# Where the transposes of a batched score kernel keep their PSUM buffers, and which engine empties which

## The chip, the cores and the metric

The kernel runs on one core of one Trainium2 chip. The time is the device time of one execution in microseconds, and the median over several executions counts. Shorter is better. The names of the engines in the profile: PE is the matrix engine (PEld its weight load), DVE the vector engine, ACT the scalar engine, POOL the GpSimd engine, SP the engine whose queue issues the transfers here.

## What is computed

```python
def reference(q: np.ndarray, k: np.ndarray) -> np.ndarray:
    scale = 1.0 / np.sqrt(q.shape[-1])
    return (np.einsum('bhqd,bhkd->bhqk', q, k) * scale).astype(np.float32)
```

q and k are f32 arrays of 8 batches, 8 heads, 512 rows and 64 columns, 8.4 MB each. The result has 8 x 8 matrices of 512 x 512 f32 scores, 67.1 MB.

## The kernel before

The work is cut into four units (`UNITS`) of two batches each. A unit's k and q arrive as one tile `big` of 128 partitions with 32 KB on each, by two transfers of 2 MB (line 78). `load_and_cast` turns each of the two into a bf16 tile `xb`, in two halves, on POOL (line 82). All four units' loads and casts stand in the program ahead of everything else. The pool of `big` tiles has three buffers, which the loads and the output tiles share in rotation: units 0 to 2 take buffers 0 to 2, unit 3 takes buffer 0 again, and the output tiles follow with 1, 2, 0 and so on. So the first output tile needs unit 1's casts to be over, the second unit 2's, and the third unit 3's; from the fourth on, each needs the store of three tiles before to have landed.

`transpose` brings the columns of k and q onto the partitions. It does so in eight groups for each unit, four for k (line 107) and four for q (line 116). A group is eight 128 x 128 transposes on PE into one PSUM tile `tp` (a pool of two), and then four copies of 64 x 512 out of it, in `rearrange` (line 95). The groups' copies go to DVE and ACT in turn. k ends up in `kT`; q ends up in `qz`, a tile padded with zeros, of which there are two for the whole kernel, cleared by DVE at the start (line 147). `transpose` is a generator: a group is five steps, one that issues the eight transposes and four that issue one copy each, 40 steps for a unit.

`scores` computes one output tile of 4 MB, the matrices of four heads of one batch: 16 matmuls of 128 x 512 (line 132), two to a PSUM tile `ps` of two banks (a pool of three), and eight evacuations, each of 128 x 1024, which multiply by the scale (`evacuate`). Of six evacuations three are on ACT (line 64) and three on DVE (line 66). Then SP stores the tile with one transfer (line 137). A unit has four such tiles (`TILES`), so there are 16 stores and 128 evacuations.

The first unit's transposes run by themselves, before any score. The next unit's are mixed into the current unit's scores by hand: after each evacuation the main loop takes one or two steps of the generator. In unit 0 it takes one step after each evacuation of the first tile and two in the later tiles; in the other units one, and two after every fourth evacuation.

Each engine executes its instructions in the order of the program (`keep_in_program_order`), and waits at one of them until what it needs is there. SP has all eight loads first, then the 16 stores.

Of the kernel before, what the change touches and what calls it, by code (L numbers as in the profile page):

```python
# [1 line left out]

# [5 lines left out]


@with_exitstack  # L10
def kernel(
    ctx: ExitStack,
    tc: tile.TileContext,
    q: bass.AP,
    k: bass.AP,
    out: bass.AP,
):

    nc = tc.nc
    B, H, S, D = q.shape
    scale = 1.0 / (D ** 0.5)
    P = 128
    UNITS = B // 2
    N = H
    M = P // (2 * H)  # L30
    R = S // M
    J = R // 2
    RO = 8
    U = S // RO
    JJ = J // RO
    IW = 8 // JJ
    TILES = N // 2

    f32 = mybir.dt.float32
    bf16 = mybir.dt.bfloat16  # L40

    q_r = q.rearrange("(v b) g (m j) d -> v (b g m) (j d)", b=2, j=R)
    k_r = k.rearrange("(v b) g (m j) d -> v (b g m) (j d)", b=2, j=R)
    out_r = out.rearrange("(v b) (t x h) (u i) k -> v (b t) (h u) x (i k)", b=2, x=2, h=2, i=RO)

    consts = ctx.enter_context(tc.tile_pool(name="consts", bufs=1))

    big_pool = ctx.enter_context(tc.tile_pool(name="big", bufs=3))
    bf_pool = ctx.enter_context(tc.tile_pool(name="bf", bufs=6))
    t_pool = ctx.enter_context(tc.tile_pool(name="t", bufs=2))  # L50
    tpsum_pool = ctx.enter_context(tc.tile_pool(name="tpsum", bufs=2, space=bass.MemoryType.PSUM))
    psum_pool = ctx.enter_context(tc.tile_pool(name="psum", bufs=3, space=bass.MemoryType.PSUM))


    pinned = tc.keep_in_program_order

    n_evac = 0
    n_tp = 0

    def evacuate(dst, src):  # L60
        nonlocal n_evac

        if n_evac % 6 in (0, 2, 3):
            pinned(nc.scalar.mul(out=dst, in_=src, mul=scale))  # L64
        else:
            pinned(nc.vector.tensor_scalar(out=dst, in0=src, scalar1=scale, scalar2=None,  # L66
                                           op0=mybir.AluOpType.mult))
        n_evac += 1

    def half(h):  # L70
        return slice(h * D, (h + 1) * D)

    def load_and_cast(v):

        xf = big_pool.tile([P, 2, 2, J * D], f32, name="big")
        both = []
        for x, src in enumerate((k_r, q_r)):
            nc.sync.dma_start(out=xf[:, x], in_=src[v].rearrange("p (s c) -> p s c", s=2))
        for x in range(2):
            xb = bf_pool.tile([P, J, 2, D], bf16, name="xb")  # L80
            for s in range(2):
                pinned(nc.gpsimd.tensor_copy(out=xb[:, :, s, :],  # L82
                                             in_=xf[:, x, s].rearrange("p (j d) -> p j d", j=J)))
            both.append(xb)
        return both

    def rearrange(tp, pattern, dst):

        nonlocal n_tp
        copy = (nc.vector.tensor_copy, nc.scalar.copy)[n_tp % 2]  # L90
        n_tp += 1
        for s in range(2):
            src = tp[half(s)].rearrange(pattern, n=N, h=2)
            for h in range(2):
                pinned(copy(out=dst(s, h), in_=src[:, h]))  # L95
                yield

    def transpose(v, kb, qb):


        kT = t_pool.tile([P, N, M, 2, J], bf16, name="kT")
        qz = qzs[v % 2]
        ts[v] = (kT, qz)
        for j0 in range(0, J, 8):
            tp = tpsum_pool.tile([P, 8, P], bf16, name="tp")
            for j in range(8):
                pinned(nc.tensor.transpose(out=tp[:, j, :], identity=identity,  # L107
                                           in_=kb[:, j0 + j].rearrange("p s d -> p (s d)")))
            yield
            yield from rearrange(tp, "d j (n h m) -> d h n m j",  # L110
                                 lambda s, h: kT[half(h), :, :, s, j0:j0 + 8])
        for i0 in range(0, RO, IW):
            tp = tpsum_pool.tile([P, IW, JJ, P], bf16, name="tp")
            for i in range(IW):
                for jj in range(JJ):
                    pinned(nc.tensor.transpose(out=tp[:, i, jj, :], identity=identity,  # L116
                                               in_=qb[:, RO * jj + i0 + i].rearrange("p s d -> p (s d)")))
            yield
            yield from rearrange(tp, "d i jj (n h m) -> d h i n m jj",
                                 lambda s, h: qz[half(h), i0:i0 + IW, :, h * U:(h + 1) * U]  # L120
                                 .rearrange("d i n (m s jj) -> d s i n m jj", s=2, jj=JJ)[:, s])

    def scores(v, t):

        kT, qz = ts[v]
        o = big_pool.tile([P, 2, RO, S], f32, name="big")
        for x in range(2):
            n = 2 * t + x
            for i in range(0, RO, 2):
                ps = psum_pool.tile([P, 2, S], f32, name="ps")  # L130
                for w in range(2):
                    pinned(nc.tensor.matmul(out=ps[:, w, :], lhsT=qz[:, i + w, n, :],  # L132
                                            rhs=kT[:, n].rearrange("d m s j -> d (m s j)"),
                                            start=True, stop=True))
                evacuate(o[:, x, i:i + 2, :], ps)
                yield
        nc.sync.dma_start(out=out_r[v, t], in_=o.rearrange("p x i k -> p x (i k)"))  # L137

    def take(steps, count):
        for _ in range(count):  # L140
            next(steps, None)

    identity = consts.tile([P, P], dtype=bf16)
    make_identity(nc, identity)
    qzs = [consts.tile([P, RO, N, P], bf16, name=f"qz{n}") for n in range(2)]
    for qz in qzs:
        nc.vector.memset(qz, 0.0)  # L147
    cast = [load_and_cast(v) for v in range(UNITS)]

    ts = {}  # L150
    for _ in transpose(0, *cast[0]):
        pass
    for v in range(UNITS):
        ahead = transpose(v + 1, *cast[v + 1]) if v + 1 < UNITS else iter(())
        for t in range(TILES):
            for n, _ in enumerate(scores(v, t)):

                take(ahead, 1 + (t > 0 if v == 0 else n % 4 == 3))
        for _ in ahead:
            pass  # L160


# [1 line left out]
_INS = ['q', 'k']  # L164
_OUTS = [((8, 8, 512, 512), 'float32')]


# [23 lines left out]
```

## Time and profile before

| | us |
|---|---|
| median of 7 executions | 203.06 (202.72 to 203.38) |
| the profiled execution | 203.25 |
| its span, from the first to the last instruction | 201.4 |
| DVE busy | 126.3 |
| PE busy | 101.5 |
| ACT busy | 100.6 |
| POOL busy | 30.5 |

The span lacks what lies around the instructions, so it is shorter than the time of the same execution. In the profile's rows of 40 digits each digit is one fortieth of the span, about 5 us, and 9 means busy for 90% or more of it; the DMA row is the mean over the core's 16 DMA engines. The DMA engines moved 83.97 MB in 5510 packets: 16.78 MB were read from the chip's memory and 67.11 MB written. In a row of the costliest groups stand the line, the engine, the operation and its shapes, the number of instructions, the busy time and the mean ns of one, and then the idle time ahead of them with what ended most of it. A line of the timeline has the start, the busy time, the engine and line, the operation, and in brackets the idle time ahead of it and what ended it.

### The profile page before, as it was taken

The page shows a single profiled execution, that of the slowest core. Times are in us where ns is not written, and L with a number is a line of the kernel's source. Part 1 is how long each engine was busy: PE and PEld are TensorE (multiplying, and loading weights), DVE is VectorE, ACT ScalarE, POOL GpSimd, SP SyncE. Part 2 cuts the span into 40 slices and gives each one's busy share as a digit, 9 for nine tenths or more (in the row PEclk, how much of TensorE's full clock was granted, in tenths as well). Part 3 has the DMA queues.
Part 4 walks back from the last instruction along what each step waited for, and adds up shares of the span by engine and source line. Part 5 has one row for each costly group of instructions (what it writes and reads, how often), then busy time and mean ns, then how long its engine had stood idle before and what let it go on. Part 6 is the DMA issues. An engine that isn't in the chain of part 4 may idle for free.

```text
span 201.4 us, 1456 instructions
## 1 busy us (share of the span) xinstructions
PE 101.5 (50%) x503; PEld 48.2 (24%) x512; DVE 126.3 (63%) x130; ACT 100.6 (50%) x129; POOL 30.5 (15%) x22
## 2 busy tenths in 40 slices
PE   0033366753868549484935554954765465710000
PEld 0033343321413224242412221421222121200000
DVE  6736659995988949796749796669456064530000
ACT  2016667795765775666758563775525341520000
POOL 1277777557000000000000000000000000000000
PEclk9999999999678996969699997599587858555555
DMA  6999999999999999999999999999999999999993
GB/s 208 442 426 426 433 436 426 416 397 439 423 433 431 431 426 429 436 426 426 439 429 426 426 439 426 426 433 429 433 433 436 416 429 429 433 426 436 433 429 153
DMA packets 5510, 83.97 MB, mean 417 GB/s; under 512 B 384, under 2 KB 384, under 8 KB 384
## 3 DMA queue, kind: packets, MB, share of 16 engines
q1 hardware_dynamic: 5504, 83.89, 98.0%
q8 instruction: 4, 0.07, 0.1%
q14 instruction: 2, 0.02, 0.0%
HBM read 16.78 MB, written 67.11 MB: 416 GB/s over the span
## 4 chain that ended last, share of the span: by engine, by line
DMA 42%; DVE 8%; PE 6%; ACT 2%; issue 1%; ACTq 0%; SPq 0%; DVEq 0%
DMA out_dram<-big 42%; DVE big L66 7%; PE ps L132 6%; ACT big L64 2%; DVE kT L95 1%; ACT qz L95 1%; PE tp L116 1%; ACTq L64 0%; SPq L137 0%; DVEq L66 0%
## 5 line engine op out<-in xcount | busy, mean ns | idle before, releaser
L132 PE MATMUL ps<-kT,qz 128*128 128x512 bf16 x247 | 83.5, 461 | 52.5 <-ACT big L64 35.3
L66 DVE TENSOR_SCALAR big<-ps 128x1024 f32<-128x1024 f32 x64 | 76.3, 1221 | 40.4 <-DMA out_dram<-big 28.2
L64 ACT ACTIVATE big<-ps 128x1024 f32<-128x1024 f32 x64 | 63.6, 1022 | 56.8 <-DMA out_dram<-big 29.1
L132 PEld LDWEIGHTS <-qz 128*128 128x128 bf16 x256 | 28.0, 112 | 96.1 <-issue 85.0
L82 POOL CAST xb<-big 128x2048 bf16<-128x2048 f32 x16 | 29.8, 1893 | 17.9 <-DMA big<-in_k_dram 9.7
L95 ACT COPY kT<-tp 64x512 bf16<-64x512 bf16 x32 | 18.5, 578 | 14.6 <-PE tp L107 14.3
L95 DVE COPY kT<-tp 64x512 bf16<-64x512 bf16 x32 | 22.0, 687 | 6.0 <-PE tp L107 5.6
L95 DVE COPY qz<-tp 64x512 bf16<-64x512 bf16 x32 | 22.0, 687 | 3.1 <-PE tp L116 2.7
L95 ACT COPY qz<-tp 64x512 bf16<-64x512 bf16 x32 | 18.5, 578 | 4.5 <-PE tp L116 4.1
L107 PE MATMUL tp<-identity,xb 128*128 128x128 bf16 x128 | 11.5, 248 | 16.9 <-POOL xb L82 12.4
L116 PE MATMUL tp<-identity,xb 128*128 128x128 bf16 x128 | 12.7, 262 | 6.2 <-DVE kT L95 3.2
L107 PEld LDWEIGHTS <-xb 128*128 128x128 bf16 x128 | 10.1, 113 | 21.0 <-POOL xb L82 12.7
L116 PEld LDWEIGHTS <-xb 128*128 128x128 bf16 x128 | 11.1, 120 | 10.8 <-issue 8.8
L147 DVE MEMSET qz<- 128x4096 uint32 x2 | 6.9, 3472 | 2.5 <-PEq L175 1.7
L95 ACT ACT_TABLE_LOAD x1 | 1.3, 1283 | 0.7 <-PEq L175 0.7
masks.py:199 POOL TENSOR_SCALAR_AFFINE_SELECT identity<-identity 128x128 bf16<-128x128 bf16 x1 | 0.3, 292 | 0.1
masks.py:197 POOL MEMSET identity<- 128x128 bf16 x1 | 0.2, 204 | 0.3 <-POOLq L175 0.3
L175 POOL MEMSET const-float32-0.0<- 128x1 f32 x1 | 0.1, 98 | 0.2 <-issue 0.2
L175 POOL MEMSET const-bfloat16-1.0<- 128x1 bf16 x1 | 0.1, 101 | 0.0
L175 POOL MEMSET const-uint8-127<- 128x1 uint8 x1 | 0.1, 101 | 0.0
L175 POOL MEMSET const-float32-1.0<- 128x1 f32 x1 | 0.1, 98 | 0.0
## 6 DMA issues: line engine op xcount, KB each, us to landing
out_dram<-big SPq DMA_DIRECT2D x16, 4096.0 KB, 21.2
big<-in_k_dram SPq DMA_DIRECT2D x4, 2048.0 KB, 19.3
big<-in_q_dram SPq DMA_DIRECT2D x4, 2048.0 KB, 24.3
```

Source lines behind the costliest of these rows:

```text
L64: pinned(nc.scalar.mul(out=dst, in_=src, mul=scale))
L66: pinned(nc.vector.tensor_scalar(out=dst, in0=src, scalar1=scale, scalar2=None, op0=mybir.AluOpType.mult))
L82: pinned(nc.gpsimd.tensor_copy(out=xb[:, :, s, :], in_=xf[:, x, s].rearrange("p (j d) -> p j d", j=J)))
L95: pinned(copy(out=dst(s, h), in_=src[:, h]))
L107: pinned(nc.tensor.transpose(out=tp[:, j, :], identity=identity, in_=kb[:, j0 + j].rearrange("p s d -> p (s d)")))
L116: pinned(nc.tensor.transpose(out=tp[:, i, jj, :], identity=identity, in_=qb[:, RO * jj + i0 + i].rearrange("p s d -> p (s d)")))
L132: pinned(nc.tensor.matmul(out=ps[:, w, :], lhsT=qz[:, i + w, n, :], rhs=kT[:, n].rearrange("d m s j -> d (m s j)"), start=True, stop=True))
L147: nc.vector.memset(qz, 0.0)
L175: nc = _bacc.Bacc("TRN2", target_bir_lowering=False, num_devices=1)
```

## The change

Six things are changed:

- The first unit's transposes use two pools: groups 0, 1, 4 and 5 take the two `tp` buffers as before, groups 2, 3, 6 and 7 take buffers of the scores' pool `ps`. All other units use `tp` alone.
- Two of every three evacuations go to ACT and one to DVE. With three `ps` buffers in rotation, a buffer is then always emptied by the same engine.
- In unit 0 the main loop takes two steps of the next unit's transposes after every evacuation, in the first tile too. The other units are as before.
- The first half of the first cast (k of unit 0) is done by DVE.
- The transposes of k and q go through one helper, `transposed`.
- The two PSUM pools are made in the other order.

```diff
--- before.py
+++ after.py
@@ -33,7 +33,6 @@
     RO = 8
     U = S // RO
     JJ = J // RO
-    IW = 8 // JJ
     TILES = N // 2
 
     f32 = mybir.dt.float32
@@ -48,8 +47,8 @@
     big_pool = ctx.enter_context(tc.tile_pool(name="big", bufs=3))
     bf_pool = ctx.enter_context(tc.tile_pool(name="bf", bufs=6))
     t_pool = ctx.enter_context(tc.tile_pool(name="t", bufs=2))
+    psum_pool = ctx.enter_context(tc.tile_pool(name="psum", bufs=3, space=bass.MemoryType.PSUM))
     tpsum_pool = ctx.enter_context(tc.tile_pool(name="tpsum", bufs=2, space=bass.MemoryType.PSUM))
-    psum_pool = ctx.enter_context(tc.tile_pool(name="psum", bufs=3, space=bass.MemoryType.PSUM))
 
 
     pinned = tc.keep_in_program_order
@@ -60,7 +59,7 @@
     def evacuate(dst, src):
         nonlocal n_evac
 
-        if n_evac % 6 in (0, 2, 3):
+        if n_evac % 3 < 2:
             pinned(nc.scalar.mul(out=dst, in_=src, mul=scale))
         else:
             pinned(nc.vector.tensor_scalar(out=dst, in0=src, scalar1=scale, scalar2=None,
@@ -79,8 +78,8 @@
         for x in range(2):
             xb = bf_pool.tile([P, J, 2, D], bf16, name="xb")
             for s in range(2):
-                pinned(nc.gpsimd.tensor_copy(out=xb[:, :, s, :],
-                                             in_=xf[:, x, s].rearrange("p (j d) -> p j d", j=J)))
+                copy = nc.vector.tensor_copy if v == x == s == 0 else nc.gpsimd.tensor_copy
+                pinned(copy(out=xb[:, :, s, :], in_=xf[:, x, s].rearrange("p (j d) -> p j d", j=J)))
             both.append(xb)
         return both
 
@@ -101,22 +100,29 @@
         kT = t_pool.tile([P, N, M, 2, J], bf16, name="kT")
         qz = qzs[v % 2]
         ts[v] = (kT, qz)
-        for j0 in range(0, J, 8):
-            tp = tpsum_pool.tile([P, 8, P], bf16, name="tp")
-            for j in range(8):
-                pinned(nc.tensor.transpose(out=tp[:, j, :], identity=identity,
-                                           in_=kb[:, j0 + j].rearrange("p s d -> p (s d)")))
+        W = 8
+
+        def transposed(rows):
+            if v == 0 and n_tp % 4 > 1:
+                tp = psum_pool.tile([P, W, P], bf16, name="ps")
+            else:
+                tp = tpsum_pool.tile([P, W, P], bf16, name="tp")
+            for w, row in enumerate(rows):
+                pinned(nc.tensor.transpose(out=tp[:, w, :], identity=identity,
+                                           in_=row.rearrange("p s d -> p (s d)")))
+            return tp
+
+        for j0 in range(0, J, W):
+            tp = transposed([kb[:, j0 + j] for j in range(W)])
             yield
             yield from rearrange(tp, "d j (n h m) -> d h n m j",
-                                 lambda s, h: kT[half(h), :, :, s, j0:j0 + 8])
+                                 lambda s, h: kT[half(h), :, :, s, j0:j0 + W])
+        IW = W // JJ
         for i0 in range(0, RO, IW):
-            tp = tpsum_pool.tile([P, IW, JJ, P], bf16, name="tp")
-            for i in range(IW):
-                for jj in range(JJ):
-                    pinned(nc.tensor.transpose(out=tp[:, i, jj, :], identity=identity,
-                                               in_=qb[:, RO * jj + i0 + i].rearrange("p s d -> p (s d)")))
+            tp = transposed([qb[:, RO * jj + i0 + i] for i in range(IW) for jj in range(JJ)])
             yield
-            yield from rearrange(tp, "d i jj (n h m) -> d h i n m jj",
+            yield from rearrange(tp.rearrange("p (i jj) c -> p i jj c", jj=JJ),
+                                 "d i jj (n h m) -> d h i n m jj",
                                  lambda s, h: qz[half(h), i0:i0 + IW, :, h * U:(h + 1) * U]
                                  .rearrange("d i n (m s jj) -> d s i n m jj", s=2, jj=JJ)[:, s])
 
@@ -155,7 +161,7 @@
         for t in range(TILES):
             for n, _ in enumerate(scores(v, t)):
 
-                take(ahead, 1 + (t > 0 if v == 0 else n % 4 == 3))
+                take(ahead, 2 if v == 0 else 1 + (n % 4 == 3))
         for _ in ahead:
             pass
 
```

## Prediction

> **What bounds the kernel now.** I read the page's DMA rows first, because the kernel moves 84 MB and does little arithmetic on it.
>
> ```profile
> DMA  6999999999999999999999999999999999999993
> q1 hardware_dynamic: 5504, 83.89, 98.0%
> DMA out_dram<-big 42%; DVE big L66 7%; PE ps L132 6%; ACT big L64 2%; DVE kT L95 1%; ACT qz L95 1%; PE tp L116 1%; ACTq L64 0%; SPq L137 0%; DVEq L66 0%
> ```
>
> The 16 DMA engines are busy in every slice from 5 us to 196 us and 98% over the span, while the busiest compute engine, DVE, has 63%. The chain of waits names stores and the evacuations released by a store's landing; it goes back only to 57.3 us, and a compute piece on it costs time only where the queue behind it ran dry. So the question is where the DMA engines do less than full work. The view by stretches (length, then PE, PEld, DVE, ACT, POOL busy, clock, DMA share, GB/s):
>
> ```profile
> 0.00:2.00 2.00, 0.00 (x0) 0.00 (x0) 0.34 (x1) 1.27 (x1) 0.70 (x6) 1.00 0.33 57
> 2.00:3.00 1.00, 0.00 (x0) 0.00 (x0) 1.00 (x1) 0.01 (x1) 0.00 (x0) 1.00 0.74 197
> 3.00:4.00 1.00, 0.00 (x0) 0.00 (x0) 1.00 (x1) 0.00 (x0) 0.00 (x0) 1.00 0.82 344
> 39.00:41.50 2.50, 1.71 (x12) 0.87 (x12) 2.44 (x4) 1.88 (x3) 2.19 (x2) 1.00 1.07 393
> ...
> 198.00:199.00 1.00, 0.00 (x0) 0.00 (x0) 0.00 (x0) 0.00 (x0) 0.00 (x0) 0.50 0.23 98
> 199.00:200.00 1.00, 0.00 (x0) 0.00 (x0) 0.00 (x0) 0.00 (x0) 0.00 (x0) 0.50 0.12 49
> 200.00:201.40 1.40, 0.00 (x0) 0.00 (x0) 0.00 (x0) 0.00 (x0) 0.00 (x0) 0.50 0.00 0
> ```
>
> Front: 2 x 0.67 + 0.26 + 0.18 = 1.8 us of idle before the queue is full. Middle: nothing idle; one dip at 39 to 41.5 us, where the queue turns from loads to stores (393 GB/s against 428 to 431 in the long stretches: 2.5 x (1 - 393/428) = 0.2 us). End: 0.77 + 0.88 + 1.40 = 3.05 us with few or no engines. A share of 0.12 is two engines of 16: most are done at about 198.3 us, two go on to 200. So the span is 1.8 + about 196.5 of transfer + 3.1 = 201.4, and the profiled execution, 203.25 us, has 1.85 us around it.
>
> The two late engines can be traced back. In the trace's landing records all 16 engines report a load within 0.8 us of each other up to 33 us. For the last q load fifteen report at 42.3 to 43.2 us and one at 45.1. It fell behind at 36.6 to 39 us, where another queue takes time on one engine:
>
> ```profile
> q1 hardware_dynamic: 79, 1.03, 94.2%
> q8 instruction: 1, 0.02, 2.6%
> ```
>
> In that window, 36.4 to 39 us, an instruction fetch of one packet takes 0.026 x 16 x 2.6 = 1.1 us of one engine. That engine was already the last by 0.5 us, loses 1.2 us here and 0.85 us more at the turn to stores, and stays some 2 us behind until it ends the kernel (last store: fourteen report by 199.6 us, one at 200.5, one at 200.6). The other late one loses about 0.2 us a store between 110 and 170 us.
>
> **The change part by part.** Its parts can only act by moving stores' issues or the casts, so each is followed to there.
>
> ```profile
> L66 DVE TENSOR_SCALAR big<-ps 128x1024 f32<-128x1024 f32 x64 | 76.3, 1221 | 40.4 <-DMA out_dram<-big 28.2
> L64 ACT ACTIVATE big<-ps 128x1024 f32<-128x1024 f32 x64 | 63.6, 1022 | 56.8 <-DMA out_dram<-big 29.1
> L82 POOL CAST xb<-big 128x2048 bf16<-128x2048 f32 x16 | 29.8, 1893 | 17.9 <-DMA big<-in_k_dram 9.7
> L95 DVE COPY kT<-tp 64x512 bf16<-64x512 bf16 x32 | 22.0, 687 | 6.0 <-PE tp L107 5.6
> L95 ACT COPY kT<-tp 64x512 bf16<-64x512 bf16 x32 | 18.5, 578 | 14.6 <-PE tp L107 14.3
> ```
>
> (1) Half a cast moves from POOL to DVE. DVE finishes its two memsets at 9.40 us; the first k load landed before 8.63. No row has this operation on DVE. Lower end: the memset's rate, 3.47 us for 4096 elements, gives 1.74 us. Upper end: the f32 evacuation, 1.22 us for 1024, gives 2.44. I take 2.44, the row that also reads f32: k is cast at 11.85 us instead of 12.36, 0.5 sooner (0.5 to 1.2).
>
> [...]
>
> (2) The first unit's eight groups of transposes rotate through more buffers. Now a pair of groups costs 4.2 us (13.49, 17.79, 21.79, 26.09 us: the starts of DVE's copies), because each waits for the copies of two groups ago; a DVE group is 4 x 0.687 = 2.75, an ACT group 4 x 0.578 = 2.31, eight transposes 0.94. With the wait gone DVE is the limit: k groups 12.9 to 18.4; q is cast at 17.24 as before, so q groups run 18.4 to 23.9. ACT is done by then too, against 29.30 now: 5.4 us sooner.
>
> (3) The first evacuation cannot use all of it. Its output tile takes the buffer of the second unit's loads, whose last cast ends at 23.30 + 3.73 = 27.03 us, set by a landing. So it starts at 27.05 instead of 29.32. With two transpose steps for each evacuation and two of three evacuations on ACT, the first tile needs of ACT 6 x 1.022 + 4 x 0.578 = 8.4 us, of DVE 2 x 1.221 + 8 x 0.687 = 7.9. First store: 35.5 to 37 us instead of 38.15. The DMA queue has loads until 1.8 + 16.78 MB / 0.4285 = 41.0 us, and from an issue to the first packet it takes about 1.1 us: the store is wanted by 39.9. It was in time and stays in time: 0 us.
>
> (4) Second store: its buffer is free at 33.09 + 3.73 = 36.82 as before; ACT owes at most 5 x 1.022 + 8 x 0.578 = 9.7 us, so 46.5 or less against 45.97 now; wanted by 41.0 + 9.8 + 0.2 - 1.1 = 49.9. 0 us.
>
> (5) Third store, the narrowest place:
>
> ```profile
> 45.26 3.73 POOL L82 CAST xb<-big 128x2048 bf16<-128x2048 f32 x2 [2.21 <-DMA big<-in_q_dram]
> 49.02 1.22 DVE L66 TENSOR_SCALAR big<-ps 128x1024 f32<-128x1024 f32 x1 [2.37 <-POOL xb L82]
> 58.49 0.37 SPq L137 DMA_DIRECT2D out_dram<-big  x1
> ```
>
> Its tile waits for the last cast, which waits for the late engine; then it took 9.5 us. Wanted by 49.9 + 9.8 = 59.7: 1.2 us to spare. DVE had 6 evacuations and 5 copies in that stretch with ACT idle for 3 us. With the next unit's transposes spread two steps at a time from the start, fewer fall into this tile: ACT has 5 x 1.022 + 4 x 0.578 = 7.4 us, DVE 3 x 1.221 + 3 x 0.687 = 5.7. Store at 56.5 to 57.5: 0 us, with more to spare.
>
> (6) From there on a tile may take two stores, 2 x 9.8 - 1.1 = 18.4 us, from a landing to its issue. Now it takes 7 to 9 (84.02 to 91.63, 171.49 to 178.40). Over the kernel ACT goes from 100.6 to 86 x 1.022 + 37.0 = 125 us, DVE from 126.3 to 42 x 1.221 + 44 + 6.9 + 2.4 = 105. A tile asks 7.8 us of ACT, 6.0 of DVE, and of PE at half clock 16 x 0.44 + 16 x 0.13 = 9.2: wholly in a row 23, the same as now (6.4 + 7.6 + 9.2), and that overlaps into 7.6 today. Cover is 9 us: 0 us. Without it a late store would cost its lateness, microsecond for microsecond.
>
> Sum: 0 on the profiled execution (203.25), which stands 0.2 over the median of 203.06. The one thing left is which engines the fetches strike and when: PE runs its program some 5 us sooner at the start, so the fetch at 36.6 us comes at about 31, still among loads. Value 0, bounds -1.4 (all engines finish together: the work of the tail spread over 16 is 0.35 us, so it ends at 198.4 instead of 199.8) and +1.3 (the last engine is struck once more, at the 1.1 to 1.3 us that one strike cost).
>
> **The rivals.** *The tail evens out* (0.18): the late engine escapes the fetch or the turn. For: it owes 2 us to two events. Against: the second late engine ends only 0.1 us before it, by another cause, so both must improve. About 202.3 us.
>
> *The third store comes late* (0.08): slower. If the new order of copies makes its tile take over 10.7 us from 49.02, the queue dries up at 60.8. For: only 1.2 us to spare, PE's clock halves at 51.6. Against: fewer steps in that tile. At 13 us it is 2.3 us late: 205.3.
>
> *One more strike on a late engine* (0.12): slower. ACT gains 22 evacuations, so one more fetch of its program is possible, and fetch times shift. One strike among 16 engines mostly misses the two that count. About 203.9.
>
> *The new buffers do nothing* (0.05, counted as no change): were the transposes to wait as now, the first store would still go by 38.15, and the time is the same.
>
> **How the numbers follow.** No change has 0.62 with that last one, 203.0 us. A difference under 0.2% (0.4 us) cannot be told from none here: the seven runs spread by 0.66. Faster 0.18, within 0.62, slower 0.20. The bounds of the fetch term give 201.7 to 204.4 at the outside; leaving out 2 in 10 gives 202.2 to 204.0.
>
> **What would show it.** Right: DMA 98% again, first store at 35.5 to 37 us, third before 58.5, ACT evacuations 86, and a tail of two engines over about 2 us. Wrong: an idle DMA slice at 60 us, or late engines that lose more or less than 2 us.

## The result: slower by 0.17%

The changed kernel takes 203.34 us (median of 22 executions, 202.93 to 203.84), the kernel before 202.90 (58 executions, 202.49 to 203.58). The ratio is 1.0017, 95% interval 1.0010 to 1.0024. That is inside the range forecast and under the 0.2% named there, but the forecast was no change, and the difference is clear of its interval: slower. A second set on another chip gave 1.0019 (1.0011 to 1.0028).

Start with what did happen as foreseen. The page of the changed kernel, rows for the DMA queue, the chain of waits and the groups of the changed work:

```profile
q1 hardware_dynamic: 5504, 83.89, 98.0%
...
DMA out_dram<-big 43%; DMA big<-in_k_dram 13%; PE ps L138 10%; ACT big L63 7%; POOL xb L82 5%; DVE big L65 4%; DVE qz L94 1%; SPq L77 1%; POOLq L192 1%; ACT kT L94 1%; ACTq L192 0%; PE tp L111 0%; ACT qz L94 0%; ACTq L63 0%; DVEq L65 0%
...
L63 ACT ACTIVATE big<-ps 128x1024 f32<-128x1024 f32 x86 | 84.5, 1023 | 43.4 <-DMA out_dram<-big 24.3
L65 DVE TENSOR_SCALAR big<-ps 128x1024 f32<-128x1024 f32 x42 | 51.4, 1225 | 67.9 <-DMA out_dram<-big 39.3
...
L82 POOL CAST xb<-big 128x2048 bf16<-128x2048 f32 x15 | 29.8, 2013 | 18.0 <-DMA big<-in_k_dram 10.8
```

The transfers still fill 98% of the span, and 22 evacuations have gone to ACT. Of these rows only the mean of POOL's casts has grown (2013 ns from 1893), by one cast at the start that is taken up below. The queue of SP, with the starts of the first three stores (start, length, what):

```profile
35.43 0.40 SPq L143 DMA_DIRECT2D out_dram<-big  x1
...
46.58 0.39 SPq L143 DMA_DIRECT2D out_dram<-big  x1
...
56.32 0.37 SPq L143 DMA_DIRECT2D out_dram<-big  x1
```

The first store is 2.7 us earlier than before, the third 2.2 us, and the view by stretches has the DMA engines at 1.01 of full work from 30 to 50 us.

The two profiled executions don't show the loss: 203.39 us for the changed kernel, 203.25 for the one before, which is 0.35 over that kernel's own median. The executions of the kernel before fall into two heaps, most at 202.6 to 203.1 us and some at 203.2 to 203.6, and its profile caught one of the second heap. So the question is not only what an execution looks like, but how often it lands in which heap. I count the executions of 203.15 us and more, and call them the upper heap: 17 of 58 before, 18 of 22 after.

### The profile page after: what moved, and what is told of

It reads as the page before. It is cut to its first block, busy times and chain, and to the rows that moved or that the text cites. A ratio compares the mean times of both kernels' runs of the same rounds, so it can differ in the third digit from the quotient of the medians.

```text
span 201.5 us, 1459 instructions
## 1 busy us (share of the span) xinstructions
PE 102.8 (51%) x503; PEld 48.9 (24%) x512; DVE 102.5 (51%) x109; ACT 121.0 (60%) x151; POOL 30.5 (15%) x21
## 4 chain that ended last, share of the span: by engine, by line
DMA 55%; PE 10%; ACT 8%; DVE 5%; POOL 5%; issue 3%; SPq 1%; POOLq 1%; ACTq 1%; DVEq 0%
DMA out_dram<-big 43%; DMA big<-in_k_dram 13%; PE ps L138 10%; ACT big L63 7%; POOL xb L82 5%; DVE big L65 4%; DVE qz L94 1%; SPq L77 1%; POOLq L192 1%; ACT kT L94 1%; ACTq L192 0%; PE tp L111 0%; ACT qz L94 0%; ACTq L63 0%; DVEq L65 0%
## 5 line engine op out<-in xcount | busy, mean ns | idle before, releaser
L63 ACT ACTIVATE big<-ps 128x1024 f32<-128x1024 f32 x86 | 84.5, 1023 | 43.4 <-DMA out_dram<-big 24.3
L65 DVE TENSOR_SCALAR big<-ps 128x1024 f32<-128x1024 f32 x42 | 51.4, 1225 | 67.9 <-DMA out_dram<-big 39.3
L82 POOL CAST xb<-big 128x2048 bf16<-128x2048 f32 x15 | 29.8, 2013 | 18.0 <-DMA big<-in_k_dram 10.8
L111 PE MATMUL tp<-identity,xb 128*128 128x128 bf16 x224 | 20.8, 250 | 15.0 <-POOL xb L82 13.6
L94 ACT COPY kT<-tp 64x512 bf16<-64x512 bf16 x28 | 16.2, 578 | 12.5 <-PE tp L111 12.2
L94 DVE COPY kT<-tp 64x512 bf16<-64x512 bf16 x28 | 19.2, 687 | 3.2 <-PE tp L111 2.9
L94 DVE COPY qz<-tp 64x512 bf16<-64x512 bf16 x28 | 19.2, 686 | 0.4
L94 ACT COPY qz<-tp 64x512 bf16<-64x512 bf16 x28 | 16.2, 578 | 0.5 <-PE tp L111 0.2
L111 PE MATMUL ps<-identity,xb 128*128 128x128 bf16 x32 | 3.8, 314 | 0.0
L94 DVE COPY kT<-ps 64x512 bf16<-64x512 bf16 x4 | 2.8, 688 | 0.1
L94 DVE COPY qz<-ps 64x512 bf16<-64x512 bf16 x4 | 2.8, 688 | 0.1
```

Of the source, the lines that this page charges most:

```text
L82: pinned(copy(out=xb[:, :, s, :], in_=xf[:, x, s].rearrange("p (j d) -> p j d", j=J)))
L111: pinned(nc.tensor.transpose(out=tp[:, w, :], identity=identity, in_=row.rearrange("p s d -> p (s d)")))
```

## The experiments

### One part of the change at a time

Each is the kernel before with one edit. Theory A: ACT's longer program needs one more fetch (an 8 KB packet at 202.49 us that the trace of the kernel before lacks). B: the first unit's transposes end earlier, so PE's fetch (28.72 us instead of 36.57) and the stores come earlier. C: the half cast on DVE.

```diff
split_only
-        if n_evac % 6 in (0, 2, 3):
+        if n_evac % 3 < 2:
cast_only
-                pinned(nc.gpsimd.tensor_copy(out=xb[:, :, s, :],
-                                             in_=xf[:, x, s].rearrange("p (j d) -> p j d", j=J)))
+                copy = nc.vector.tensor_copy if v == x == s == 0 else nc.gpsimd.tensor_copy
+                pinned(copy(out=xb[:, :, s, :], in_=xf[:, x, s].rearrange("p (j d) -> p j d", j=J)))
steps_only
-                take(ahead, 1 + (t > 0 if v == 0 else n % 4 == 3))
+                take(ahead, 2 if v == 0 else 1 + (n % 4 == 3))
psum_only (and the order of the two pools, and the helper)
+            if v == 0 and n_tp % 4 > 1:
+                tp = psum_pool.tile([P, W, P], bf16, name="ps")
```

> The kernel before with one edit: two of three evacuations on ACT. Theory A (ACT's program has grown past a length at which one more piece of it is fetched, seen in the changed kernel as an 8 KB instruction packet at 202.5 us): slower by 0.3 to 0.45 us, a ratio of 1.0015 to 1.002, and a third 8 KB packet late in the trace. Theory B (the first unit's transposes end earlier, so PE fetches its program at 28.7 us instead of 36.6, and the stores are issued earlier): ratio 1.000 within 0.0007, the fetch stays near 36 us. Theory C (the half cast on DVE beside POOL's): 1.000.

> The kernel before with one edit: the first half of the first cast on DVE. Theory C: slower by 0.3 us or more, with POOL's first cast stretched from 1.89 to about 3.7 us as in the changed kernel. Theories A and B: ratio 1.000 within 0.0007, since the cast ends within 0.2 us of where it did.

> The kernel before with one edit: two transpose steps for each evacuation in unit 0's first tile too. Theory B in its part on the fetch: PE's first fetch comes 1 to 3 us sooner than 36.6, some of the 0.35 us may show (ratio 1.0000 to 1.0015). Theories A and C: 1.000 within 0.0007.

> The kernel before with the first unit's transposes in the scores' PSUM buffers too, evacuations, steps and casts as before. Theory B: slower by 0.2 to 0.4 us (ratio 1.001 to 1.002), first fetch of PE at 29 to 32 us, first store at about 36 us. Theories A and C: 1.000 within 0.0007.

Measured: split 203.21 us, ratio 1.0009 (1.0000 to 1.0019); cast 203.26, 1.0009 (1.0001 to 1.0018); steps 202.97, 0.9997 (0.9988 to 1.0006); psum 203.23, 1.0013 (1.0004 to 1.0021). The psum edit, which was meant to test B, has the largest ratio. But the intervals of split, cast and psum all reach 1.0017, so this round does not say how the loss is shared among them. A and C are answered by kernels further down that keep both the longer ACT program and the half cast and show no loss (0.9998 and 0.9997). What told more was an accident: the kernel with only the steps changed issues its first store *later* than the kernel before. Here are the first store and the two microseconds in which the queue turns from loads to stores, from the view by stretches (the last two columns are DMA share and GB/s). Before, the first store:

```profile
38.15 0.40 SPq L137 DMA_DIRECT2D out_dram<-big  x1
```

and its turn:

```profile
40.00:42.00 2.00, 1.17 (x4) 0.48 (x5) 1.94 (x4) 1.41 (x3) 2.00 (x2) 1.00 0.92 319
```

After the whole change (first store at 35.43 us, above):

```profile
40.00:42.00 2.00, 1.69 (x14) 0.87 (x12) 1.89 (x2) 1.98 (x3) 2.00 (x2) 1.00 1.03 385
```

With the first unit's transposes in the scores' buffers alone, the first store in SP's queue:

```profile
34.56 0.40 SPq L143 DMA_DIRECT2D out_dram<-big  x1
```

and its turn:

```profile
40.00:42.00 2.00, 1.80 (x4) 0.50 (x4) 1.96 (x3) 1.86 (x3) 2.00 (x2) 0.50 0.98 360
```

With the steps alone, the first store:

```profile
39.46 0.40 SPq L137 DMA_DIRECT2D out_dram<-big  x1
```

and its turn:

```profile
40.00:42.00 2.00, 1.83 (x21) 1.36 (x21) 1.97 (x4) 1.49 (x3) 2.00 (x2) 1.00 1.02 434
```

The DMA engines are busy for 0.92 to 1.03 in all four, but in three they move 319 to 385 GB/s there and in the last 434; over 39 to 43 us, which takes in the stretches beside it, the difference is smaller, 393 to 397 against 422. The packet records agree: the median packet of 16 KB takes 0.611 us over the whole kernel, and at this turn 14, 14 and 12 packets take 0.7 to 1.75 us, in the last kernel none. I call a turn with such packets dirty and one without clean. The dirty turn hurts the engine that is already late most. In the landing records it is 1.8 us behind the median before the turn and 2.6 to 2.7 behind after it in the kernels before and after; with the steps alone it is 1.65 us behind on both sides.

### Holding the first store

That gave theory D: the loss is the moment of the first store. (The changed kernel's turn is no dirtier than that of the kernel before, though its store comes 2.7 us sooner; this is taken up at the end.) To test it without the rest, the changed kernel keeps everything and its first store is held: POOL, once through with unit 2's casts, makes copies on a scratch tile and then copies one column of the output tile onto itself; unit 3's casts follow. The diff has five copies of 256 columns; the others have none, eleven, and, on the kernel before, nine. (The lines that part the loads from the casts and make the scratch tile are left out.)

```diff
+        if v == t == 0:
+            for _ in range(5):
+                pinned(nc.gpsimd.tensor_copy(out=held_bf, in_=held))
+            pinned(nc.gpsimd.tensor_copy(out=o[:, 1, RO - 1, S - 1:], in_=o[:, 1, RO - 1, S - 1:]))
+            cast[3] = cast_unit(3, cast[3])
         nc.sync.dma_start(out=out_r[v, t], in_=o.rearrange("p x i k -> p x (i k)"))
```

> The changed kernel, with the first store held until POOL is through with unit 2's casts (about 38.4 us instead of 35.4) by a copy of one column onto itself; unit 3's casts stand behind it. Theory D (new): the time depends on when the first store is issued against the end of the loads, at about 41 us. A store that stands in the queue directly behind the last load makes the turn from reading to writing slow, 0.15 to 1.0 us of longer packets on each engine and most on the engine that is late; one that comes as the loads run out (39.46 us in the kernel with only the steps changed) finds no slow packets. At 38.4 us it is still in front of that point: ratio to the kernel before 1.0005 to 1.002, slow packets at 39.5 to 42 us. Theories A (longer ACT program), B (early fetch of PE): the hold changes nothing, 1.001 to 1.002.

> The same with five copies of 256 columns in front of the held store: about 40.0 us. Theory D: no packets over 0.7 us at the turn, the late engine gets about 1.4 instead of 2.3 us behind the median, and the changed kernel's loss is gone: ratio 0.9985 to 1.0003. Theories A and B: 1.001 to 1.002 as without the hold, since the program's length and the fetch at about 29 us are the same.

> The same with eleven copies: about 42 us. Theory D: clean turn, but the 15 engines in time stand idle 1 to 2 us; the second late engine (0.4 us behind at that point, 1.9 at the end) then ends the kernel, so about 1 us longer than with 40 us, ratio 1.003 to 1.007. Theories A and B: the same loss from idling on top of 1.0015.

> The kernel before with the first store held to about 40 us instead of 38.15 in the same way (nine copies). Theory D: its turn, too, becomes clean in every run, ratio 0.998 to 1.000. Theories A and B: nothing to gain, 1.000 within 0.0007, or a small loss where the queue runs dry.

Measured, with the store's real moment: changed kernel at 38.26 us 203.29 us, 1.0017 (1.0008 to 1.0026); at 40.38 us 203.12, 1.0014 (1.0005 to 1.0022); at 43.36 us 205.95, 1.0151 (1.0137 to 1.0165); kernel before at 41.05 us 203.56, 1.0027 (1.0015 to 1.0040). POOL's copies took 0.45 us each, more than I had reckoned, so the kernel before came 1.0 and the longest hold 1.4 us later than meant. D came out half right. At 40.38 us the turn was clean and the late engine's 1.7 us did not grow, as expected, and the executions moved together (203.03 to 203.20); but the time fell by only 0.17 us where the whole loss was to go. The kernel before held to 41.05 us was to gain and lost 0.27%. In the kernel held to 43.36 us the queue simply ran dry, as the stretch ahead of the store shows:

```profile
41.00:43.00 2.00, 1.93 (x8) 0.73 (x6) 1.94 (x4) 1.95 (x3) 1.75 (x5) 0.50 0.33 139
```

That suggested a valley (theory D2): too early is dirty, too late is idle, and the floor has to lie between 38.3 and 40. The records bear out "too late" but "idle" only for the longest hold. By the packet records the 16 engines together are unused for 37 us around the turn of the kernel held to 43.36 us, which is 2.3 us each, for 2.7 us at 41.05 and for 0.1 us at 40.38. What all three do show is a slower pace behind the turn: the mean report of the 16 engines moves by 9.81 to 9.84 us from store to store, against 9.76 in the changed kernel, and there are 15 such steps. Why is open. Finer holds, and the kernel before under another name as a control (the diff is the same, with one copy of 64 columns, two of 128 and four of 256):

> The changed kernel with its first store held by one copy of 64 columns: issue at about 38.5 us. Theory D2 (the time has a valley over the moment of the first store: too early gives a slow turn and a time that scatters, too late gives idle engines; before's 38.15 us lies on the early edge, its executions on both sides of it): somewhere between the 203.29 us of the hold to 38.3 and the valley, median 202.9 to 203.2. Theory E (the hold is of no account, the loss is the changed kernel's own): 203.25 as with 38.3.

> The same held by two copies of 128 columns: issue at about 38.9 us. Theory D2: in the valley, 202.8 to 203.0 us, ratio 0.9995 to 1.0008, executions within 0.25 us of each other. Theory E: ratio 1.0012 or more.

> The kernel before with its first store held by four copies of 256 columns: issue at about 38.8 us instead of 38.15. Theory D2: the executions over 203.2 us that the kernel before shows go, median 202.7 to 202.9, ratio 0.9985 to 0.9998, no packets over 0.7 us at the turn. Theory E: ratio 1.000 within 0.0006 and the same scatter.

> The kernel before once more, under a label of its own, for a second profile of it and as a measure of what a ratio can tell: 1.000 within 0.0008 by every theory. Theory D2: if its profiled execution takes under 203.0 us, its turn has few or no packets over 0.7 us; if over 203.2 us, it has many, as in the first profile.

Measured: changed kernel at 38.33 us 203.22 us, 1.0017 (1.0008 to 1.0025); at 38.65 us 202.81, 0.9998 (0.9989 to 1.0006). These two kernels differ only in the size and number of POOL's small copies. Here are the first store and the turn of the first:

```profile
38.33 0.40 SPq L152 DMA_DIRECT2D out_dram<-big  x1
40.00:42.00 2.00, 2.00 (x12) 1.29 (x11) 1.61 (x2) 1.98 (x3) 2.00 (x2) 0.51 0.95 328
```

and of the second:

```profile
38.65 0.40 SPq L152 DMA_DIRECT2D out_dram<-big  x1
40.00:42.00 2.00, 1.69 (x14) 0.87 (x12) 1.96 (x3) 1.98 (x4) 2.00 (x2) 1.00 1.07 434
```

A third of a microsecond at the store took 0.41 us from the median. That speaks against theory E for the changed kernel, though not yet by itself, as the control shows. Several expectations missed. The first came out 0.02 us above the range of D2, and the executions of the second spread over 0.55 us where 0.25 was expected. The kernel before, held to 38.68 us, gained nothing (202.96, 1.0004, 0.9995 to 1.0013): three of its eleven executions stayed over 203.15 us, and its profile still has one packet of 1.13 us at the turn. And the kernel before against itself came out at 1.0011 (1.0003 to 1.0020), 203.20 us, six of eleven in the upper heap, beside five of 33 for the same kernel in the same set. The interval of a ratio does not hold this drift of an unchanged kernel, which is about 0.1%, more than half the loss to be explained, and as large as the ratios of split and cast. A pair of kernels apart by 0.41 us is little beyond it (0.36 us); what counts is whether the order repeats.

### The same again on one chip, and by the kernel's own order

So the changed kernel and its held form ran side by side, with a third that has the old split of the evacuations, and a probe that stores the last half tile in transfers of 15, 14, 13 down to 1 partitions and 8.

```diff
oldsplit_hold39 (on the held form)
-        if n_evac % 3 < 2:
+        if n_evac % 6 in (0, 2, 3):
probe (on the held form, last tile)
+            nc.sync.dma_start(out=out_r[v, t][:, 0], in_=src[:, 0])
+            p0 = 0
+            for n in (*range(15, 0, -1), 8):
+                nc.sync.dma_start(out=out_r[v, t][p0:p0 + n, 1], in_=src[p0:p0 + n, 1])
+                p0 += n
```

> The changed kernel once more, beside its held form on one chip. Theory D2 and theory E alike: 203.2 to 203.45 us, ratio 1.001 to 1.0025. If it came out at 1.000 to 1.0006, the loss itself would be no more than the scatter between sessions (the kernel before, under another label, gave 1.0011).

> The held form (first store at about 38.7 us) once more. Theory D2: 0.2 to 0.5 us less than the changed kernel beside it, median 202.7 to 203.0 us. Theory E (no effect of the hold, the first result was scatter): the same median as the changed kernel within 0.15 us.

> The held form with the evacuations split between ACT and DVE as before. Theory A2 (ACT's longer program costs some 0.08 us outside the span: time less span is 1.87 us in every profile built on the changed kernel, 1.78 in those built on the one before): time less span 1.77 to 1.79 us, and a median 0.05 to 0.12 us below the held form's. Without theory A2: 1.86 to 1.88 us and the same median.

> The held form, its last tile stored as one transfer of half the tile and sixteen of 15, 14, 13 down to 1 and then 8 partitions, to learn which of the 16 DMA engines are the two late ones. [...]

Measured: changed kernel 203.42 us, 1.0019 (1.0011 to 1.0028), ten of eleven executions in the upper heap; held to 38.96 us 202.96, 0.9997 (0.9988 to 1.0006), none of eleven. The turn of the first, from the view by stretches:

```profile
40.00:42.00 2.00, 1.71 (x12) 0.82 (x11) 1.96 (x3) 1.98 (x3) 2.00 (x2) 0.70 0.99 360
```

and the first store of the second, in SP's queue:

```profile
38.96 0.40 SPq L152 DMA_DIRECT2D out_dram<-big  x1
```

and its turn:

```profile
40.00:42.00 2.00, 2.00 (x12) 1.16 (x11) 1.46 (x3) 1.98 (x3) 2.00 (x2) 0.50 1.08 459
```

The late engine of the first goes from 1.7 to 3.1 us behind the median at the turn, that of the second stays at 1.8, and their last reports come at 201.01 and 200.37 us: 0.64 us between the two profiles, 0.46 between the medians. The order has repeated, so the changed kernel's loss goes when one store is held; and it is the store's moment and not the rest of the hold, since the same hold to 38.26 and 38.33 us took nothing away. The held form keeps ACT's longer program and the half cast on DVE and does not lose, so neither carries the loss. The old split gave 202.96 us, 1.0001 (0.9992 to 1.0010), and time less span 1.78 us against 1.88: the first half of A2 as expected, the second, a lower median, not seen. The probe (213.27 us, one execution) settled nothing: packets of its small transfers took up to 4.2 us, so the late engines could not be told from the rest.

The last pair moves the first store by the kernel's own order, four steps after each evacuation of the first tile, and stores part of the last tile by 120 partitions to relieve one DMA engine.

```diff
after_steps4 (on the changed kernel)
-                take(ahead, 2 if v == 0 else 1 + (n % 4 == 3))
+                take(ahead, (2 if t else 4) if v == 0 else 1 + (n % 4 == 3))
relief15 (on the held form, last tile)
+            for x, p0, p1 in ((1, 0, 120), (1, 120, P), (0, 0, P)):
+                nc.sync.dma_start(out=out_r[v, t][p0:p1, x], in_=src[p0:p1, x])
```

> The changed kernel with four instead of two transpose steps after each evacuation of unit 0's first tile, and no hold: ACT has six copies more ahead of the tile's last evacuation (6 x 1.02 + 10 x 0.58 = 11.9 us from 27.0), so the first store is issued at 38.8 to 39.5 us by itself. Theory D2: the loss is gone without any held store, ratio 0.9993 to 1.0008. Theory E: 1.0015 to 1.002.

> The held form (first store at about 38.8 us) with the second half of its last tile stored by 120 partitions on 15 DMA engines and 8 partitions on 8, so that one engine gets 8 packets (4.9 us) less and eight get one packet (0.6 us) more. Theory F (two late engines set the end): if the engine without packets is a late one, the last report comes 0 to 0.7 us sooner and the ratio is 0.997 to 1.000; if neither late one is that engine, the end moves by 0 (late ones among those with equal load) or +0.6 us (one among the eight), ratio 0.9998 to 1.003. If the end were set by all engines alike, +0.6 us in any case.

Measured: four steps 202.84 us, 0.9992 (0.9983 to 1.0001), the first store in SP's queue:

```profile
39.47 0.40 SPq L143 DMA_DIRECT2D out_dram<-big  x1
```

and its turn, in the view by stretches:

```profile
40.00:42.00 2.00, 1.30 (x12) 0.84 (x12) 1.94 (x4) 1.89 (x4) 2.00 (x2) 1.00 1.02 434
```

Six more copies on ACT in the first tile, and its ratio lies 1.0017 - 0.9992 = 0.0025 under the changed kernel's; against the kernel before the interval just reaches 1, so that it beats both is not shown. The relief failed: 207.55 us, 1.0221 (1.0207 to 1.0235). Its trace has 407 packets under 512 bytes, 23 more than the 384 of 24 transfers by 16 engines, as 15 engines for the 120 partitions and 8 for the 8 give. Two stretches of it, before and after the 120-partition transfer starts:

```profile
170.00:185.00 15.00, 4.42 (x10) 1.28 (x9) 2.45 (x2) 5.81 (x6) 0.00 (x0) 0.54 1.01 429
190.00:198.00 8.00, 0.00 (x0) 0.00 (x0) 0.00 (x0) 0.00 (x0) 0.00 (x0) 0.50 0.98 270
```

Equally busy, 270 GB/s instead of 429. That swamps what one relieved engine could show, so theory F stays untested by it.

### The profiles in one table

"Long" counts 16 KB packets over 0.7 us between 39 and 43.5 us. "Behind" is the last engine's report behind the median one, for the last k load and the last q load, on the two sides of the turn. "Upper" counts executions of 203.15 us and more, "profiled" is the time of the one execution that the columns before it come from.

| kernel | first store | long | behind | last report | profiled | upper | median |
|---|---|---|---|---|---|---|---|
| psum_only | 34.56 | 12 | 1.43, 2.39 | 200.47 | 203.08 | 9 of 11 | 203.23 |
| after_again | 35.21 | 16 | 1.74, 3.14 | 201.01 | 203.73 | 10 of 11 | 203.42 |
| changed kernel | 35.43 | 14 | 1.77, 2.68 | 200.69 | 203.39 | 18 of 22 | 203.34 |
| split_only | 36.34 | 15 | 1.65, 2.74 | 200.61 | 203.24 | 7 of 12 | 203.21 |
| cast_only | 38.09 | 16 | 1.50, 2.40 | 200.40 | 203.00 | 8 of 12 | 203.26 |
| kernel before | 38.15 | 14 | 1.78, 2.63 | 200.61 | 203.25 | 17 of 58 | 202.90 |
| before_again | 38.16 | 8 | 1.64, 2.65 | 200.61 | 203.22 | 6 of 11 | 203.20 |
| after_hold38 | 38.26 | 18 | 1.75, 2.72 | 200.58 | 203.27 | 9 of 11 | 203.29 |
| after_hold385 | 38.33 | 15 | 1.76, 2.64 | 200.59 | 203.29 | 6 of 11 | 203.22 |
| after_hold39 | 38.65 | 3 | 1.57, 2.47 | 200.56 | 203.25 | 2 of 11 | 202.81 |
| before_hold387 | 38.68 | 1 | 1.60, 2.00 | 200.59 | 203.20 | 3 of 11 | 202.96 |
| oldsplit_hold39 | 38.95 | 0 | 1.87, 1.84 | 200.36 | 202.96 | 3 of 11 | 202.96 |
| after_hold39_again | 38.96 | 0 | 1.81, 1.78 | 200.37 | 203.08 | 0 of 11 | 202.96 |
| steps_only | 39.46 | 0 | 1.65, 1.65 | 200.21 | 202.81 | 1 of 11 | 202.97 |
| after_steps4 | 39.47 | 0 | 1.95, 1.93 | 200.13 | 202.74 | 2 of 11 | 202.84 |
| after_hold40 | 40.38 | 0 | 1.72, 1.70 | 200.38 | 203.08 | 2 of 11 | 203.12 |
| before_hold40 | 41.05 | 0 | 0.58, 1.49 | 201.08 | 203.69 | 6 of 6 | 203.56 |
| after_hold42 | 43.36 | 0 | 1.80, 1.79 | 203.39 | 206.08 | 4 of 4 | 205.95 |

Read down the columns for the store and the long packets: 38.33 us and earlier, 8 to 18 long packets; 38.65 and 38.68, three and one; from 38.95, none. The kernel before stands 0.2 us ahead of the last dirty one. (In before_hold40 the fetch fell between the two loads, so its 0.58 is from before the strike. The profiles of the probe and of relief15, whose ends are not comparable, have no long packet with the store at 38.82 us and three at 38.81.)

Read down the store and the median: leaving out the two rows of the kernel before, the seven rows with a store up to 38.33 us have medians of 203.21 us and more, the six from 38.65 to 39.47 us 202.97 and less. The drift of one row could be as large as that gap, but not all thirteen would fall on their side of it by drift. The kernel before does not fit: with a store at 38.15 us and a dirty turn in both profiles it has 202.90 us (203.20 in its second row), where its neighbours at 38.09 and 38.26 us have 203.26 and 203.29.

The heaps are not clean and dirty turns either. The profiled executions of cast_only (203.00 us) and psum_only (203.08) lie in the lower heap with 16 and 12 long packets. They differ from the other profiles with eight long packets or more in how far behind the last engine is after the turn, 2.4 us instead of 2.6 to 3.1.

## Why the prediction was wrong

**What bounds the kernel, the late engines, the tail: right.** 98%, two engines in the last 2 us, and the struck engine lost 1.53 us to the fetch against 1.55 before. My 1.2 us for that strike was a misreading: the landing records keep two engines 0.5 us behind right through it, so the struck engine was not the one already last but one only 0.23 us behind, and a strike costs more than the 1.1 to 1.3 us of my upper bound. For the second late engine, the second-last report goes from 1.25 us behind the median at 112 us to 2.05 at 171, over six stores 0.13 us each and not 0.2. (Two sums are off by rounding, without effect: 2 x 9.8 - 1.1 is 18.5, 16 x 0.44 + 16 x 0.13 is 9.1.)

**The times of steps (2) to (5): right to within 0.7 us.** First unit's copies done at 24.6 us (forecast 23.9), first evacuation at 26.99 (27.05), stores at 35.43, 46.58 and 56.32, each just outside its range (35.5 to 37; 46.5 or less; 56.5 to 57.5). ACT 121.0 us and DVE 102.5 are a little under the 125 and 105, since overlapping instructions count once in a busy time (ACT's evacuations: 86 x 1.023 = 88.0 us against 84.5 busy).

**Step (3), the price: the step that failed.** "It was in time and stays in time: 0 us." The moment was right, the price of 0 was not. I asked only whether the store came late. It can also come too early: a store queued right behind the last loads gave a dirty turn in every profile up to 38.33 us and none from 38.95 on, and with the rest of the changed kernel kept, holding the store into that gap took 0.41 and 0.46 us off its median, the whole loss: against the kernel before the held forms have 0.9998 and 0.9997. The turn did stand in the prediction, as a dip of 0.2 us and as 0.85 us on the late engine, but as a fixed cost that the change could only lessen. So a term that I put at nothing is worth some 0.4 us.

What is shown is that the loss goes when the store comes between 38.65 and 39.5 us, not that it came with the 2.7 us by which the change made the store earlier. Held back to 38.26 us, later than in the kernel before, the changed kernel lost as much as ever (1.0017), and the whole change's turn has no more long packets than the one before it (14 and 14). Why the kernel before, on the same dirty side, mostly escapes the price stays open.

**Step (1): mis-sized, without effect.** I bounded the half cast on DVE at 1.74 to 2.44 us; it took 1.16, less than the 1.22 that half as many f32 elements take from PSUM. Both bounds were estimates from other operations, the memset and the evacuation; what makes the cast faster than either was not shown. In the timeline of the changed kernel (start, length, engine, line, operation):

```profile
8.54 3.69 POOL L82 CAST xb<-big 128x2048 bf16<-128x2048 f32 x1 [7.24 <-DMA big<-in_k_dram]
9.32 1.16 DVE L82 CAST xb<-big 128x2048 bf16<-128x2048 f32 x1
12.28 3.33 PEld L111 LDWEIGHTS <-xb 128*128 128x128 bf16 x32 [12.28 <-POOL xb L82]
```

POOL's half, 1.89 us elsewhere, took 3.69 while DVE's ran, and the transposes began at 12.28 us, 0.13 sooner than before instead of 0.5. POOL had started 0.78 us earlier and lost 1.80 us, more than the 1.16 that DVE's cast lasted; whether DVE lost anything too can't be told, since no run has its cast without POOL's beside it. The kernel with the cast edit alone showed the same (3.57 us on POOL). The cause was not shown: beside DVE's memset, which ran to 9.40 us, POOL's first cast in the kernel before took as long as the others (all sixteen 1.890 to 1.894 us). The first evacuation did not depend on it: it started at 26.99 us, set by a landing, as forecast.

**Step (6) and the fetch: right.** Nothing starved, PE's fetch came at 28.7 us (about 31) with the same cost (a packet of 1.10 us in both kernels). ACT did get one more piece of program, as the rival had it (the 8 KB packet at 202.49 us), but 1 us behind the span's end.

**The rivals: none was this.** A late store was one of them, a store too early was not. "The tail evens out" named the turn and looked only at the side of gain.

**What stays open.** Why a store behind loads slows packets was not shown, only when. What an execution in the lower heap of the kernel before looks like is not known: both its profiles caught the upper heap, and two other kernels show that a dirty turn can end in the lower one. That the late engines set the end rests on the landing records; the two tries to shift load away from them failed for other reasons. The records do speak for it: the mean report of the 16 engines for the last store is 198.83 us in the changed kernel, 198.82 in after_hold39_again and 198.89 in the kernel before, and only the last engine's distance behind that mean differs, 1.86, 1.55 and 1.73 us.

## What to carry to other kernels

When one queue serves loads first and stores after, "earlier" need not be free for the first store: here a store held by a third of a microsecond was worth 0.4 us of 203. In a kernel bound by transfers look at the packets at the turn, and try that issue where the loads run out. A remedy that takes a loss away is not yet its cause: put the old moment back as well, and see whether the old time returns. Price every event that a change moves from both sides, too late and too early. And where a kernel's executions fall into two heaps, count heaps over several sets, with the unchanged kernel among them, before believing a difference of a tenth of a per cent.

## What the runs showed of the hardware that was not expected

- With half of the last tile stored by 120 and 8 partitions, the packet records have 105 of the 344 packets of 16 KB behind 185 us at 0.7 to 2.1 us, while the median stayed at 0.61; the rate fell from 429 to 270 GB/s.
- A dirty turn with eight long packets or more cost the late engine 0.85 to 1.4 us; the kernel got back 0.41 and 0.46 us when the store was held. The engines together catch up: their mean report of the last load is 0.2 us later in the changed kernel than in after_hold39_again (42.72 and 42.50 us), that of the last store the same.
- With the first store at 40.38 us or later the stores behind it took longer (9.81 to 9.84 us from one to the next by the mean report, 9.75 to 9.78 with the first store at 39.47 us or earlier).
- In ten of the twelve profiles with two thirds of the evacuations on ACT, the time outside the span was 1.86 to 1.90 us; in these ACT's last program fetch came 0.96 to 0.99 us after the span's end. In the other two it came 0.6 us after, and the time outside was 1.78 and 1.81, as without that fetch (1.78 to 1.81). So some 0.09 us of the changed kernel's loss may lie here; the link is not tested, and the held kernels had it too with medians of 202.81 and 202.96 us.
